# A transformer block on one core: the bias table built earlier, and the last five blocks accumulated onto terms that ScalarE writes into PSUM

## The chip, the core and the metric

The kernel runs on one core of a Trainium2 chip. The core has TensorE (matrix multiply, called PE in the profile, its weight loads PEld), VectorE (DVE), ScalarE (ACT), GpSimd (POOL) and SyncE (SP), which work side by side and wait for each other by semaphores. Data lies in SBUF, in PSUM (eight banks of 512 float32 values in each of 128 partitions, into which TensorE writes) and in device memory, reached by DMA. DMAs are issued by SyncE, ScalarE and GpSimd, each in the order of its queue. The metric is the device time of one execution in microseconds.

## The reference

One block of width 2048 on a sequence of 512 positions, all in float32. With the sizes given, only the first of four mixers is used, attention with a sliding window:

```python
hn = rmsnorm(x, norm_g[0])
q, k, v, gate = split(hn @ swa_w_in)              # 32 query heads, 4 key heads, head size 64
bias = rel_bias[bucket]                           # by distance, 32 buckets, window of 128
scores = q @ k.T * 64 ** -0.5 + bias              # masked to the window
m = maximum(scores.max(-1), sink)
probs = exp(scores - m) / (exp(scores - m).sum(-1) + exp(sink - m))
x = x + ((probs @ v) * silu(gate)) @ swa_w_out
emb = p[0] @ ple_proj
g = sigmoid(rmsnorm(x, ple_norm[0]) @ ple_gate)
x = x + emb * g
return rmsnorm(x, final_g)
```

`rel_bias` holds 32 values for each head; `bucket` maps a distance to one of 32 buckets. The products with `swa_w_out` and `ple_gate` are 512x2048 by 2048x2048.

## The kernel before

**Products.** Each float32 operand is split into a high part of fewer mantissa bits (type float32r) and the rest, and a product is made of three matmuls, high by high, high by low and low by high (`mm3`, lines L121 to L126). ScalarE makes the high part by a copy, VectorE the low part by a subtraction (L107 and L113 for the projections' weights, L709 and L710 later).

**First stage (L186 to L246).** Sixteen steps of k load a slice of x (transposed) and of the first weight columns, split both and accumulate keys, values and two chunks of queries in eight PSUM banks. Between steps 3 and 6 four row tiles of x are read into the four buffers of the pool `whole` (`quarter`), and ScalarE sums their squares (L237). At step 9 the row statistics `rstd1` go through device memory (`rdram`, L241) to a copy `rb` in all partitions (L242); both transfers are on GpSimd's queue. `rb` scales the queries and keys when they leave PSUM (L257, L280).

**The bias table (L318 to L331).** Behind the first stage's last steps GpSimd reads `rel_bias` into a quarter buffer (`misc`), fills a row of 384 values per head by a memset and 17 copies, and writes it to device memory (`tdram`). `load_bias` (L378), on SyncE's queue, reads from there the shifted rows of a group of heads into the tile `bias`. That tile belongs to a pool which takes over the room of the first stage's weights.

**Attention (the loop at L995, 16 steps for each of four key heads).** The order of all engines is written out by hand. In each step TensorE's remaining projection matmuls (`ksteps`) fill the gaps between scores, transposes and weighted sums. SyncE loads the next weights (`W.load`, L101), three buffers ahead, and between them copies weight blocks in device memory (`sum_weights`, L672), onto which GpSimd's queue adds others (L674). Their sums serve the next stage.

**The two large products.** They are computed by a scheme with seven instead of eight block products, on two levels. Of the second (`ple_gate`) the rows of the two lower row tiles (t = 2 and 3) and the columns 0 to 1023 (two chunks jj) come last: product number 4. What has been summed up for them stands, with the wrong sign, in the SBUF tile `s2`, so that their value is product minus `s2`.

**The last five blocks (L1461 to L1553).** Order by hand on all engines. A block (jj, tb) is 24 matmuls into one bank (three for each of 8 slices), and six more that make the embedding `e` in another bank. `block` then has VectorE subtract: `s2 = bank - s2` (L1479); `gated` has ScalarE take the sigmoid (L1302), VectorE multiply by `e` (L1304), add to x (L1308), and an engine sum the squares. The fourth block is cut into two halves of 256 columns. For the last half the subtraction is made on TensorE: two matmuls with a negated identity (`minus`, L1490) bring in the two parts of `-s2` (`less`, L1491 and L1492) ahead of the others (L1468). Banks come from the tags "s" and "p", two each, which the products before have left. Between the blocks stand the final norm of rows already complete and their stores; behind the last one its sum of squares, an inverse root, the scaling of the last row tile and its stores (L1555 to L1585).

Of the kernel before, what the change touches and what calls it, by code (L numbers as in the profile page):

```python
# [11 lines left out]
F32 = mybir.dt.float32  # L12
F32R = mybir.dt.float32r
# [7 lines left out]
P = 128  # L21
KC = D // P
NB = S // P
HEADS = 32
# [9 lines left out]
BUCKETS = 32  # L34
MAX_DIST = 128
WINDOW = 128
PLE = 256
EPS = 1e-6
MASKED = -3.0e38
TOEP = 384  # L40
# [15 lines left out]
def trunk_kernel(ctx: ExitStack, tc: tile.TileContext, a: dict):  # L56
    nc = tc.nc
# [63 lines left out]
    def mm3(ps, sh, sl, mh, ml, first, last, more=False):  # L121


        nc.tensor.matmul(ps, sh, mh, start=first, stop=False, skip_group_check=more)  # L124
        nc.tensor.matmul(ps, sh, ml, start=False, stop=False, skip_group_check=more)  # L125
        nc.tensor.matmul(ps, sl, mh, start=False, stop=last, skip_group_check=more)  # L126
# [3 lines left out]
    ident = const.tile([P, P], F32, name="ident")  # L130
# [24 lines left out]
    def run(gen):  # L155
        for _ in gen:
            pass
# [16 lines left out]

    kinds, upto = [], {"q": 2, "g": 0}
    for kind in "qq" + "qqqqggg" * (KVH - 1) + "ggggggg":
        kinds.append((kind, upto[kind]))
# [6 lines left out]
    for k in range(KC):  # L186
        both = start_pool.tile([P, 2, 768], F32R, tag="w0s", name=f"w0s{k}")
        wh, wl = both[:, 0], both[:, 1]
        xg = start_pool.tile([P, S + 1], F32, tag="xr", name=f"xr{k}")
        nc.sync.dma_start(xg, a["xT"][k * P : (k + 1) * P, :])  # L190
        xr, g1 = xg[:, :S], xg[:, S:]
        w0 = w0s[0] if k == 0 else start_pool.tile([P, 768], F32, tag="w0", name=f"w0_{k}")
        cuts = [slice(512, 768), slice(0, 512)] if k == 0 else [slice(0, 768)]
        for c in cuts[-1:]:
            nc.sync.dma_start(w0[:, c], a["w_first"][k][:, c])
        room = acts if k < KC // 2 else more
        h = room.tile([P, S], F32R, tag="ah", name=f"xh{k}")
        l = room.tile([P, S], F32R, tag="al", name=f"xl{k}")
        nc.scalar.mul(h, xr, g1)
# [12 lines left out]
        qc = [slice(512 + t * P, 512 + (t + 1) * P) for t in range(2)]  # L212
        if f:
            for n, (sw, mx) in enumerate(((wh, h), (wl, h), (wh, l))):
                for t in range(2):
                    nc.tensor.matmul(q_ps[t], sw[:, qc[t]], mx, start=n == 0, stop=False)
        else:
            for t in range(2):
                mm3(q_ps[t], wh[:, qc[t]], wl[:, qc[t]], h, l, f, e)
        for t in range(2):  # L220
            c = slice(t * P, (t + 1) * P)
            mm3(kt_ps[t], wh[:, c], wl[:, c], h, l, f, e)
        for t in range(NB):
            c = slice(t * P, (t + 1) * P)

            for part in "hl" if f else "lh":
                if part == "h":
                    nc.tensor.matmul(v_ps[t], h[:, c], both[:, :, 256:512], start=f, stop=e, skip_group_check=True)  # L228
                else:
                    nc.tensor.matmul(  # L230
                        v_ps[t][:, :256], l[:, c], wh[:, 256:512], start=False, stop=False, skip_group_check=True
                    )
        if 3 <= k < 3 + NB:
            t = k - 3
            xn = quarter(f"xn{t}").rearrange("p k t -> p (k t)")
            nc.sync.dma_start(xn, a["x"][t * P : (t + 1) * P, :])
            nc.scalar.activation(xn, xn, AF.Square, accum_out=ssq1[:, t : t + 1])  # L237
        if k == 9:
            run(rsqrt_mean(rstd1, ssq1, D, "r1"))
            rdram = tc.dram_tile([NB, P], F32, name="rdram")  # L240
            nc.gpsimd.dma_start(rdram.rearrange("t p -> p t"), rstd1)  # L241
# [72 lines left out]
        )  # L314
    split(V[0], values[0])


    misc = quarter("misc")  # L318
    relb, tvec = misc[:HEADS, 1, :BUCKETS], misc[:HEADS, 2, :TOEP]
    nc.gpsimd.dma_start(relb, a["rel"])  # L320
    nc.gpsimd.memset(tvec, MASKED)
    exact = BUCKETS // 2
    bk = bucket_of(np.arange(WINDOW))
    nc.gpsimd.tensor_copy(tvec[:, P - 1 : P - 1 + exact], relb[:, :exact])
    for b in range(exact, BUCKETS):
        d = np.nonzero(bk == b)[0]
        if len(d):
            lo, n = P - 1 + int(d.min()), len(d)
            nc.gpsimd.tensor_copy(tvec[:, lo : lo + n], relb[:, b : b + 1].to_broadcast([HEADS, n]))
    tdram = tc.dram_tile([HEADS, TOEP], F32, name="tdram")  # L330
    nc.gpsimd.dma_start(tdram, tvec)  # L331

    pre.close()
    banks_s.close()
# [247 lines left out]
    def blk(t):  # L582
        return slice(t * P, (t + 1) * P)
# [9 lines left out]
    def block(nm, r, c, jj, m):  # L593
        return a[nm][2 * (c - 1) + jj, 4 * (r - 1) + m]
# [462 lines left out]
    late = pool("late", reuse_waits="tile")  # L1057
# [189 lines left out]
    for at, step in enumerate(OUT):  # L1247
        if at == 20:
            order.close()
        if step == "n":  # L1250
            next(inner)
            step, p = seen, None
            seen += 1
        elif step == "m":
            next(inner2)
            step, p = ("m", seen2), None
# [3 lines left out]
        else:  # L1260
            p, jj, m = step
# [76 lines left out]
    s2, s7 = partial("s2"), partial("s7")  # L1338
# [68 lines left out]
    for at, step in enumerate(PLE, len(OUT)):  # L1407
# [7 lines left out]
        elif step[0] == "e":  # L1415
            while later:
                later.pop(0)()
            p, jj = step[1:]
# [4 lines left out]
        else:  # L1423
            p, jj, m = step
# [32 lines left out]
    ps = psums[3, 1]  # L1457
# [3 lines left out]
    w = [B.get(at_ple["e", 4, jj]) for jj in range(2)]  # L1461
    f = ple_forms.made[4]

    def block(jj, tb, tag, e_tag, c=slice(0, 512), less=None):

        ps = bank(f"last{jj}_{tb}_{c.start}", tag)
        for n, v in enumerate(less or ()):
            nc.tensor.matmul(ps[:, c], minus, v, start=n == 0, stop=False)  # L1468
        for k in range(8):
            fh, fl = f[k // 2]  # L1470
            bh, bl = B.made[at_ple[4, jj] + k // 2]
            mm3(ps[:, c], fh[:, k % 2, blk(tb)], fl[:, k % 2, blk(tb)], bh[k % 2][:, c], bl[k % 2][:, c], k == 0 and not less, k == 7)
        e_ps = embed(2 + tb, w[jj], e_tag, c)
        z = s2[:, jj, tb, c]

        def opened():
            if less:
                return gated(2 + tb, jj, ps[:, c], z, e_ps, c)
            nc.vector.tensor_sub(z, ps[:, c], z)  # L1479
            return gated(2 + tb, jj, z, z, e_ps, c)  # L1480

        return opened


    two = gate(3, 1, ps, e)
    for g in two:
        next(g)
    minus = late.tile([P, P], F32R, name="minus")
    less = [late.tile([P, 256], F32R, name=f"less{n}") for n in range(2)]
    nc.scalar.mul(minus, ident, -1.0)  # L1490
    nc.scalar.copy(less[0], s2[:, 1, 1, 256:])  # L1491
    nc.vector.tensor_sub(less[1], s2[:, 1, 1, 256:], less[0].bitcast(F32))  # L1492
    for g in two:
        next(g)
    split_last(7)
# [44 lines left out]
    g = block(1, 1, "p", "t", slice(0, 256))()  # L1540
    next(g)
    by_gain(3, 0)
    next(g)
# [5 lines left out]
    last = block(1, 1, "s", "o", slice(256, 512), less)()  # L1549
    n += 1  # L1550
    next(last)
    next(last)
# [80 lines left out]
```

## Time and profile before

| | us |
|---|---|
| median of 3 runs | 792.78 |
| lowest and highest | 791.22, 794.69 |
| the profiled execution | 791.03 |
| its span, first to last instruction | 789.3 |

In a list of instructions a row gives the start and the duration in us, the engine, the line of the kernel, the operation, what it writes and reads, shapes, how many were merged (x), and in brackets how long the engine had been idle before and what ended that. In a list of waits a row gives who waited for whom, the total in us, how often, and the longest. In a table by stretches of time the columns are the stretch, the busy time of PE, PEld, DVE, ACT and POOL with their number of instructions, the granted TensorE clock as a share of full speed, the DMA engines' share and GB/s. A trailing q (SPq) marks an engine's issuing part. A matmul's end is modelled, and matmuls overlap, so the distance of two starts tells its cost, not its duration.

### The profile page before, as it was taken

How to read it: one execution, taken by the hardware profiler on the slowest of the kernel's cores; microseconds unless marked ns; L12 is line 12 of the kernel's file. 1: busy time of each engine (PE TensorE's matmuls, PEld its weight loads, DVE VectorE, ACT ScalarE, POOL GpSimd, SP SyncE). 2: the span in 40 equal slices, each digit the busy share in tenths (PEclk: the TensorE clock that was granted, in tenths of full speed). 3: DMA queues.
4: the chain of work that ended last, by engine and by line, in shares of the span. 5: the costliest groups of instructions: out<-in, count | busy, mean ns of one | idle time of the engine just before them, and what ended most of it. 6: DMA issues, size and time to landing. Idle time of an engine off the chain costs nothing.

```text
span 789.3 us, 11284 instructions
## 1 busy us (share of the span) xinstructions
PE 778.5 (99%) x3726; PEld 650.0 (82%) x3726; DVE 623.7 (79%) x1056; ACT 506.5 (64%) x1024; POOL 180.4 (23%) x394
## 2 busy tenths in 40 slices
PE   9999999999999999999999999999999999999995
PEld 8888788888888888888888888888888888888885
DVE  4446468887977788787886798999798988999686
ACT  5632366667666666565665655767788857967465
POOL 0002423544344414444143300200000021101000
PEclk9999999999999999999999999999999999999998
DMA  8797799999999999989997497998778999967833
GB/s 332 282 251 189 259 280 331 297 290 300 305 312 245 309 268 275 278 212 246 294 245 208 136 352 288 245 367 281 249 272 248 365 238 251 255 227 215 256 117 118
DMA packets 50634, 206.99 MB, mean 262 GB/s; under 512 B 7264, under 2 KB 8416, under 8 KB 44208
## 3 DMA queue, kind: packets, MB, share of 16 engines
q1 hardware_dynamic: 40240, 156.15, 54.7%
q0 software_dynamic: 9904, 49.61, 32.8%
q8 instruction: 29, 0.48, 0.2%
q10 hardware_dynamic: 432, 0.52, 0.2%
q14 instruction: 29, 0.24, 0.1%
HBM read 199.38 MB, written 78.69 MB: 352 GB/s over the span
## 4 chain that ended last, share of the span: by engine, by line
PE 92%; DMA 3%; DVE 2%; ACT 1%; issue 1%; SPq 0%; POOL 0%; ACTq 0%; DVEq 0%; POOLq 0%
PE gps L124 7%; PE gps L125 7%; PE gps L126 7%; PE qps L124 6%; PE qps L125 5%; PE qps L126 5%; PE g L125 5%; PE o L124 5%; PE g L124 5%; PE g L126 5%; PE o L125 5%; PE o L126 5%; DMA wraw<-in_w_q 2%; PE vps L228 2%; PE s L400 2%; PE o L522 2%
## 5 line engine op out<-in xcount | busy, mean ns | idle before, releaser
L124 PE MATMUL gps<-xh,whi 128*128 128x512 f32 x256 | 100.5, 393 | 0.0
L125 PE MATMUL gps<-xl,whi 128*128 128x512 f32 x256 | 100.1, 391 | 0.0
L126 PE MATMUL gps<-xh,wlo 128*128 128x512 f32 x256 | 99.9, 390 | 0.0
L113 DVE TENSOR_TENSOR wlo<-wraw,whi 128x1024 fp32r<-128x1024 f32 x60 | 74.6, 1246 | 30.5 <-ACT whi L107 17.2
L502 POOL TENSOR_SCALAR_AFFINE_SELECT own<-r 64x256 fp32r<-64x256 f32 x96 | 60.1, 626 | 162.2 <-DVE r L491 82.7
L126 PE MATMUL qps<-xh,wlo 128*128 128x512 f32 x224 | 87.5, 391 | 0.5 <-DVE wlo L113 0.5
L124 PE MATMUL qps<-xh,whi 128*128 128x512 f32 x224 | 87.7, 391 | 0.0
L125 PE MATMUL qps<-xl,whi 128*128 128x512 f32 x224 | 87.5, 391 | 0.0
L460 ACT ACTIVATE t<-t,sm 128x129 f32<-128x129 f32 x128 | 50.7, 397 | 51.7 <-DVE sm L451 48.8
L107 ACT CAST whi<-wraw 128x1024 fp32r<-128x1024 f32 x60 | 62.2, 1038 | 20.9 <-DMA wraw<-in_w_q 20.9
L710 DVE TENSOR_TENSOR blo<-braw,bhi 128x1024 fp32r<-128x1024 f32 x43 | 52.7, 1229 | 14.9 <-ACT bhi L709 14.9
L709 ACT CAST bhi<-braw 128x1024 fp32r<-128x1024 f32 x43 | 45.0, 1050 | 28.9 <-DMA braw<-in_ple_gate 9.5
L710 DVE TENSOR_TENSOR blo<-ring,bhi 128x1024 fp32r<-128x1024 f32 x48 | 58.3, 1223 | 4.7 <-ACT bhi L709 4.3
L709 ACT CAST bhi<-ring 128x1024 fp32r<-128x1024 f32 x48 | 50.2, 1049 | 17.9 <-PE o L126 14.1
L124 PE MATMUL g<-bhi,fhg 128*128 128x512 f32 x148 | 58.0, 392 | 0.0
L125 PE MATMUL g<-blo,fhg 128*128 128x512 f32 x148 | 57.8, 391 | 0.0
L126 PE MATMUL g<-bhi,flg 128*128 128x512 f32 x148 | 57.7, 390 | 0.0
L126 PEld LDWEIGHTS gps<-xh,wlo 128*128 128x128 f32 x256 | 48.1, 188 | 10.5
L124 PEld LDWEIGHTS gps<-xh,whi 128*128 128x128 f32 x256 | 48.1, 188 | 9.1
L483 ACT CAST r<-pt 128x256 fp32r<-128x256 f32 x64 | 23.8, 371 | 49.5 <-PE pt L478 49.3
L125 PEld LDWEIGHTS gps<-xl,whi 128*128 128x128 f32 x256 | 48.1, 188 | 8.6
L126 PEld LDWEIGHTS qps<-xh,wlo 128*128 128x128 f32 x224 | 42.1, 188 | 10.0 <-DVE wlo L113 1.0
(303 smaller groups left out, 2034.4 us busy)
## 6 DMA issues: line engine op xcount, KB each, us to landing
w_out<-in_w_out POOLq DMA_DIRECT2D x32, 512.0 KB, 9.2
wraw<-in_w_gate_in SPq DMA_DIRECT2D x32, 512.0 KB, 7.7
ring<-w_out SPq DMA_DIRECT2D x32, 512.0 KB, 4.7
wraw<-in_w_q SPq DMA_DIRECT2D x28, 512.0 KB, 9.3
braw<-in_ple_gate SPq DMA_DIRECT2D x22, 512.0 KB, 5.2
ring<-in_w_out SPq DMA_DIRECT2D x18, 512.0 KB, 5.5
ple_gate<-in_ple_gate SPq DMA_DIRECT2D x16, 512.0 KB, 10.0
ple_gate<-in_ple_gate POOLq DMA_DIRECT2D x16, 512.0 KB, 7.9
```

What stands on the lines that cost most here:

```text
L107: nc.scalar.copy(hi, self.raw[i])
L113: nc.vector.tensor_sub(lo, raw, hi.bitcast(F32))
L124: nc.tensor.matmul(ps, sh, mh, start=first, stop=False, skip_group_check=more)
L125: nc.tensor.matmul(ps, sh, ml, start=False, stop=False, skip_group_check=more)
L126: nc.tensor.matmul(ps, sl, mh, start=False, stop=last, skip_group_check=more)
L228: nc.tensor.matmul(v_ps[t], h[:, c], both[:, :, 256:512], start=f, stop=e, skip_group_check=True)
L400: nc.tensor.matmul(s_ps[:, u, : 2 * n], st, key[:, :, first : first + n], start=True, stop=True)
L460: nc.scalar.activation(su, su, AF.Exp, bias=sm[:, u : u + 1], accum_out=sm[:, 2 + u : 3 + u])
L483: nc.scalar.copy(r[:, 0], PT[i])
L502: nc.gpsimd.affine_select(out=cols(own[places[g % 2 ^ low]]), in_=cols(r[here, low].bitcast(F32)), pattern=[[sign * QB, 2], [0, GROUP], [s ...
L709: nc.scalar.copy(hi, raw)
L710: nc.vector.tensor_sub(lo, raw, hi.bitcast(F32))
```

## The change

The bias table becomes a function, `bias_table`, called at step 8 of the first stage; its instructions are the same. In the last five blocks, `seed` has ScalarE write `-s2` into the block's bank ahead of its matmuls, all of which accumulate (no matmul of the block starts the bank anew). The subtraction on VectorE, the negated identity, the two `less` tiles and their two matmuls are gone, and every sigmoid reads PSUM. A seed is issued a block ahead, the two half blocks' seeds together.

```diff
+    def bias_table():
+        misc = quarter("misc")
+        relb, tvec = misc[:HEADS, 1, :BUCKETS], misc[:HEADS, 2, :TOEP]
+        nc.gpsimd.dma_start(relb, a["rel"])
+        nc.gpsimd.memset(tvec, MASKED)
...
+        nc.gpsimd.dma_start(tdram, tvec)
+        return tdram
...
+        if k == 8:
+            tdram = bias_table()
         if k == 9:
             run(rsqrt_mean(rstd1, ssq1, D, "r1"))
...
-    def block(jj, tb, tag, e_tag, c=slice(0, 512), less=None):
-
-        ps = bank(f"last{jj}_{tb}_{c.start}", tag)
-        for n, v in enumerate(less or ()):
-            nc.tensor.matmul(ps[:, c], minus, v, start=n == 0, stop=False)
+    seeded = {}
+
+    def seed(jj, tb, tag, c=slice(0, 512)):
+
+        ps = seeded[jj, tb, c.start] = bank(f"last{jj}_{tb}_{c.start}", tag)
+        nc.scalar.mul(ps[:, c], s2[:, jj, tb, c], -1.0)
+
+    def block(jj, tb, e_tag, c=slice(0, 512)):
+
+        ps = seeded[jj, tb, c.start]
         for k in range(8):
...
-            mm3(ps[:, c], fh[:, k % 2, blk(tb)], fl[:, k % 2, blk(tb)], bh[k % 2][:, c], bl[k % 2][:, c], k == 0 and not less, k == 7)
+            mm3(ps[:, c], fh[:, k % 2, blk(tb)], fl[:, k % 2, blk(tb)], bh[k % 2][:, c], bl[k % 2][:, c], False, k == 7, True)
         e_ps = embed(2 + tb, w[jj], e_tag, c)
         z = s2[:, jj, tb, c]
-            nc.vector.tensor_sub(z, ps[:, c], z)
-            return gated(2 + tb, jj, z, z, e_ps, c)
+        return gated(2 + tb, jj, ps[:, c], z, e_ps, c)
...
-    minus = late.tile([P, P], F32R, name="minus")
-    less = [late.tile([P, 256], F32R, name=f"less{n}") for n in range(2)]
-    nc.scalar.mul(minus, ident, -1.0)
-    nc.scalar.copy(less[0], s2[:, 1, 1, 256:])
-    nc.vector.tensor_sub(less[1], s2[:, 1, 1, 256:], less[0].bitcast(F32))
+    seed(0, 0, "s")
...
     next(root)
-    g = block(0, 0, "s", "o")()
+    seed(1, 0, "s")
+    g = block(0, 0, "o")
...
-    g = block(1, 0, "s", "t")()
+    seed(0, 1, "p")
+    g = block(1, 0, "t")
...
     next(root)
-    g = block(0, 1, "p", "o")()
+    seed(1, 1, "p", slice(0, 256))
+    seed(1, 1, "s", slice(256, 512))
+    g = block(0, 1, "o")
```

What moves, engine by engine; names are the program's tiles, with a number that tells buffers apart. GpSimd's queue from the first stage's end, before:

```order
L241 DMA rdram_481<-rstd1_143 128x4x1
L242 DMA rb_91<-rdram_481 128x512
L674 DMA ple_gate_5_0_0_746<-in_ple_gate 64x2048
L674 DMA ple_gate_5_0_1_747<-in_ple_gate 64x2048
L674 DMA ple_gate_5_0_2_748<-in_ple_gate 64x2048
L674 DMA ple_gate_5_0_3_749<-in_ple_gate 64x2048
L320 DMA misc_715<-in_rel 32x32
L321 MEMSET misc_715 32x384
L324 COPY misc_715<-misc_715 32x16
```

The same queue after the change, from the table's last copies on:

```order
L190 COPY misc_437<-misc_437 32x12
L190 COPY misc_437<-misc_437 32x14
L190 COPY misc_437<-misc_437 32x15
L192 DMA tdram_459<-misc_437 32x384
L261 DMA rdram_503<-rstd1_143 128x4x1
L262 DMA rb_91<-rdram_503 128x512
L679 DMA ple_gate_5_0_0_746<-in_ple_gate 64x2048
```

The table now stands ahead of the statistics' two transfers and of the four accumulating transfers, behind which it stood.

ScalarE ahead of the first of the last blocks, before (`bhi129` is a projection weight's high part, `z1_0` a sigmoid's output, `last7` the high part of a weight of the last product):

```order
L709 CAST bhi128_7605<-braw128_7560 128x1024
L1302 ACTIVATE z1_0_7643<-g1_1_0_6515,rstd2_6389 128x512
L709 CAST bhi129_7623<-braw129_7582 128x1024
L1302 ACTIVATE z1_1_7644<-g1_1_1_6516,rstd2_6389 128x512
L1490 ACTIVATE minus_7647<-ident_83 128x128
L1491 CAST less0_7648<-s2_6395 128x256
L717 CAST last7_7657<-grown86_6702 128x1024
L1311 ACTIVATE z1_0_7643,ssq3_5026<-x1_3_5021 128x512
L1311 ACTIVATE z1_1_7644,ssq3_5026<-x1_3_5021 128x512
L167 ACT_TABLE_LOAD
L167 ACTIVATE rt_r3_7667<-ms_r3_7666 128x2
L1302 ACT_TABLE_LOAD
```

ScalarE at the same place after (`last0_0_0` and `last1_0_0` are PSUM banks):

```order
L714 CAST bhi128_7605<-braw128_7560 128x1024
L1307 ACTIVATE z1_0_7643<-g1_1_0_6515,rstd2_6389 128x512
L714 CAST bhi129_7623<-braw129_7582 128x1024
L1307 ACTIVATE z1_1_7644<-g1_1_1_6516,rstd2_6389 128x512
L1474 ACTIVATE last0_0_0_7647<-s2_6395 128x512
L722 CAST last7_7653<-grown86_6702 128x1024
L1316 ACTIVATE z1_0_7643,ssq3_5026<-x1_3_5021 128x512
L1316 ACTIVATE z1_1_7644,ssq3_5026<-x1_3_5021 128x512
L167 ACT_TABLE_LOAD
L167 ACTIVATE rt_r3_7663<-ms_r3_7662 128x2
L1474 ACTIVATE last1_0_0_7668<-s2_6395 128x512
L1307 ACT_TABLE_LOAD
```

The first seed stands where the negated identity stood, behind two casts and two sigmoids; the second stands behind the square root.

TensorE where the first of the last blocks begins, before, with what an instruction waits for:

```order
L124 MATMUL e_127_0_7634<-bhi_7584,pTh 128x512
L125 MATMUL e_127_0_7634<-blo_7585,pTh 128x512
L126 MATMUL e_127_0_7634<-bhi_7584,pTl 128x512
L124 MATMUL last_0_0_7672<-spare,fhg_00_7425 128x512
L125 MATMUL last_0_0_7672<-spare,fhg_00_7425 128x512
```

and after:

```order
L124 MATMUL e_127_0_7634<-bhi_7584,pTh 128x512
L125 MATMUL e_127_0_7634<-blo_7585,pTh 128x512
L126 MATMUL e_127_0_7634<-bhi_7584,pTl 128x512
L124 MATMUL last_0_0_7647<-spare,fhg_00_7425 128x512 [waits Activation_49]
L125 MATMUL last_0_0_7647<-spare,fhg_00_7425 128x512
```

The order is the same; the block's first matmul now waits for ScalarE. The same wait stands at the first matmul of each of the other four blocks.

More of the change, by code (lines that the diff above doesn't have):

```diff
@@ L173, in rsqrt_mean @@
         nc.vector.tensor_mul(out, y, t)
+    def bias_table():
[3 more added lines that the diff above has]
+        nc.gpsimd.memset(tvec, MASKED)
+        exact = BUCKETS // 2
+        bk = bucket_of(np.arange(WINDOW))
+        nc.gpsimd.tensor_copy(tvec[:, P - 1 : P - 1 + exact], relb[:, :exact])
+        for b in range(exact, BUCKETS):
+            d = np.nonzero(bk == b)[0]
+            if len(d):
+                lo, n = P - 1 + int(d.min()), len(d)
+                nc.gpsimd.tensor_copy(tvec[:, lo : lo + n], relb[:, b : b + 1].to_broadcast([HEADS, n]))
+        tdram = tc.dram_tile([HEADS, TOEP], F32, name="tdram")
+        nc.gpsimd.dma_start(tdram, tvec)
+        return tdram
     kinds, upto = [], {"q": 2, "g": 0}
@@ L315, in trunk_kernel @@
     split(V[0], values[0])
[L318 to L331, printed above, removed]
     pre.close()
@@ L1471, in block @@
             bh, bl = B.made[at_ple[4, jj] + k // 2]
-            mm3(ps[:, c], fh[:, k % 2, blk(tb)], fl[:, k % 2, blk(tb)], bh[k % 2][:, c], bl[k % 2][:, c], k == 0 and not less, k == 7)
+            mm3(ps[:, c], fh[:, k % 2, blk(tb)], fl[:, k % 2, blk(tb)], bh[k % 2][:, c], bl[k % 2][:, c], False, k == 7, True)
         e_ps = embed(2 + tb, w[jj], e_tag, c)
         z = s2[:, jj, tb, c]
-        def opened():
-            if less:
-                return gated(2 + tb, jj, ps[:, c], z, e_ps, c)
-            nc.vector.tensor_sub(z, ps[:, c], z)
-            return gated(2 + tb, jj, z, z, e_ps, c)
-        return opened
+        return gated(2 + tb, jj, ps[:, c], z, e_ps, c)
     two = gate(3, 1, ps, e)
@@ L1539, in trunk_kernel @@
     base, ms, ys, nw, yn = (const.tile([P, 1], F32, name=f"{v}_3") for v in ("base", "ms", "ys", "nw", "yn"))
-    g = block(1, 1, "p", "t", slice(0, 256))()
+    g = block(1, 1, "t", slice(0, 256))
     next(g)
@@ L1548, in trunk_kernel @@
     nc.vector.tensor_mul(x1[1][:, 3, :256], x1[1][:, 3, :256], gain(1)[:, :256])
-    last = block(1, 1, "s", "o", slice(256, 512), less)()
+    last = block(1, 1, "o", slice(256, 512))
     n += 1
```

## The prediction

> **What bounds the kernel now.** I read the page's busy times first, then its chain of waits, then what TensorE itself waited for. These are the three:
>
> ```profile
> PE 778.5 (99%) x3726; PEld 650.0 (82%) x3726; DVE 623.7 (79%) x1056; ACT 506.5 (64%) x1024; POOL 180.4 (23%) x394
> ```
>
> ```profile
> PE 92%; DMA 3%; DVE 2%; ACT 1%; issue 1%; SPq 0%; POOL 0%; ACTq 0%; DVEq 0%; POOLq 0%
> ```
>
> ```profile
> PE warm_ps L145 <- PEq L1623: 0.8, 1, 0.8
> PE qps L126 <- DVE wlo L113: 0.5, 1, 0.5
> PE o L524 <- POOL own L502: 0.3, 1, 0.3
> PE qps L216 <- ACT xh L199: 0.2, 1, 0.2
> ```
>
> TensorE is busy for 99% of the span and its waits add up to 1.8 us. Of these only two (0.5 and 0.3) lie where the change works. So the span is the sum of the matmuls, plus what stands behind the last one:
>
> ```profile
> 780.05 0.28 PE L126 MATMUL e<-bhi,pTl 128*128 128x256 f32 x1
> ```
>
> ```profile
> 780.44 0.42 DVE L1304 TENSOR_TENSOR s<-e,s 128x256 f32<-128x256 f32 x1 [0.37 <-PE e L126]
> ```
>
> The last matmul ends at 780.33. VectorE had idled 0.37 us for it, so the end of about 9 us up to 789.3 hangs on TensorE's last matmul and on nothing earlier. Whatever delays or shortens TensorE's stream before it moves the end one for one; work on VectorE or ScalarE counts only where TensorE waits for it.
>
> **First part, the table.** Rows of GpSimd, of ScalarE's first row sum, of VectorE's first use of the row statistics rb, of SyncE, SyncE's total wait, and TensorE's last matmul of the first stage:
>
> ```profile
> 37.68 0.95 POOL L241 DMA_DIRECT2D rdram<-rstd  x1 [36.30 <-DVE rstd L173]
> ...
> 65.78 0.80 POOL L320 DMA_DIRECT2D misc<-in_rel  x1
> ...
> 78.02 2.08 POOL L329 COPY misc<-misc 32x3 f32<-32x3 f32 x16
> ```
>
> ```profile
> 13.71 1.92 ACT L237 ACTIVATE xn<-xn 128x2048 f32<-128x2048 f32 x1 [1.69 <-DMA xn<-in_x]
> ```
>
> ```profile
> 68.56 1.44 DVE L257 TENSOR_TENSOR rawq<-qps,rb 128x256 f32<-128x256 f32 x4 [4.91 <-PE qps L126]
> ```
>
> ```profile
> 51.55 3.46 SPq L672 DMA_DIRECT2D ple_gate<-in_ple_gate  x4
> 82.36 0.72 SPq L378 DMA_DIRECT2D bias<-tdram  x1
> 83.15 0.87 SPq L101 DMA_DIRECT2D wraw<-in_w_q  x2
> ```
>
> ```profile
> SPq L378 <- DMA tdram<-misc: 27.2, 1, 27.2
> ```
>
> ```profile
> 71.58 0.40 PE L228 MATMUL vps<-w0s,xh 128*128 128x512 f32 x1
> ```
>
> The table takes one small read, a memset, 17 copies and one write, all on GpSimd's queue. It now takes over the quarter buffer of the first row tile, which the square frees at about 15.7. With the 12.2 us from its read to the copies (65.78 to 78.02) and 2.1 us of copies it is complete at about 30, over 7 us ahead of the queue's next item, the statistics' transfer at 37.68. Were the read twice as slow, that transfer would start some 5 us late; its result, rb, is first read at 68.56, and there VectorE had waited 4.91 us for TensorE, not for rb. Price: nothing, covered by GpSimd's 36.3 us of idle time, and if that cover were short, by those 4.9. The accumulating ple_gate transfers behind it on that queue wait for their own copies, past 61. The copies' 2 us beside VectorE's first-stage work fall where that engine is under half busy.
>
> What it frees is SyncE. It stood from 55.0 (51.55 plus 3.46) to 82.36 at the bias load, 27.2 us, with the weight loads queued behind it. The load keeps one other condition, the room of the first stage's weights, which TensorE reads last at 71.58 plus 0.40. So SyncE moves on at about 72, some 10 us sooner. What the late loads cost TensorE:
>
> ```profile
> 87.01 1.05 ACT L107 CAST whi<-wraw 128x1024 fp32r<-128x1024 f32 x1 [13.07 <-DMA wraw<-in_w_q]
> ```
>
> ```profile
> 88.09 1.23 DVE L113 TENSOR_TENSOR wlo<-wraw,whi 128x1024 fp32r<-128x1024 f32 x1 [11.91 <-PE qps L125]
> ```
>
> ```profile
> 88.45 0.40 PE L125 MATMUL qps<-xl,whi 128*128 128x512 f32 x1
> 89.37 0.51 PE L126 MATMUL qps<-xh,wlo 128*128 128x512 f32 x1 [0.53 <-DVE wlo L113]
> ```
>
> Matmuls of 512 columns start 0.23 us apart in this trace (752.34 and 752.57 below). Here the step is 0.92, so 0.69, about 0.7 us, are lost, and ten microseconds more of lead remove all of it. The 0.3 us at own (L502) come from crowded engines some 40 us later; whether earlier loads thin them out the trace doesn't tell, so I count half. Gain: 0.7 plus 0.15 is 0.85, between 0 (another wait takes the place) and 1.0.
>
> **Second part, the seeds.** Five ScalarE writes into PSUM replace four subtractions on VectorE (L1479), one negated identity, one cast and one subtraction for the last half block, and two matmuls (L1468). The two matmuls stand in the chain itself:
>
> ```profile
> 776.50 0.24 PE last L1468 x2
> ```
>
> Gain: 0.24. VectorE's four subtractions (three of 512 columns, one of 256) gain nothing by themselves: the tail above shows it waiting for TensorE. But the seeds bring five waits to TensorE, each at a block's first matmul, with the rest of the stream queued behind it. Before, that matmul needed only a free bank. The first one meets these rows:
>
> ```profile
> 750.63 1.05 ACT L709 CAST bhi<-braw 128x1024 fp32r<-128x1024 f32 x1 [3.69 <-DMA braw<-in_ple_proj]
> 751.58 0.68 ACT L1302 ACTIVATE z<-g,rstd 128x512 f32<-128x512 f32 x1
> 752.16 1.04 ACT L709 CAST bhi<-braw 128x1024 fp32r<-128x1024 f32 x1
> 753.10 0.69 ACT L1302 ACTIVATE z<-g,rstd 128x512 f32<-128x512 f32 x1
> 753.68 0.30 ACT L1490 ACTIVATE minus<-ident 128x128 fp32r<-128x128 f32 x1
> ```
>
> ```profile
> 752.34 0.39 PE L124 MATMUL last<-spare,fhg 128*128 128x512 f32 x1
> 752.57 0.39 PE L125 MATMUL last<-spare,fhg 128*128 128x512 f32 x1
> ```
>
> ```profile
> L570 ACT ACTIVATE gps<-gate x16: 593/602/604, 162.4 to 454.2; 128x512 f32<-128x512 f32 x16
> ```
>
> The seed takes the place of L1490 in ScalarE's queue, behind two casts and two sigmoids that began only when a projection weight landed. So it starts at 753.68. Its price is that of the nearest form in the trace, a 128x512 write from SBUF to PSUM with a constant scale: 0.60 (L570). It is done at 754.28, and TensorE was ready at 752.34. Loss: 1.94 us.
>
> The second seed follows the square root:
>
> ```profile
> 759.52 0.20 ACT L167 ACTIVATE rt_r<-ms_r 128x2 f32<-128x2 f32 x1
> ```
>
> ```profile
> 759.14 0.39 PE L124 MATMUL last<-last,fhg 128*128 128x512 f32 x1
> ```
>
> It ends near 760.2. Alone that would hold TensorE back by 1.1 us, but the first wait has already moved the need from 759.14 to 761.08: covered, and if that cover went, 1.1 us would appear instead. For the third I followed both queues on: it is ready near 766, needed at about 768. The two half seeds are ready near 773.4, needed at about 774.7 and 778.3. So the waits don't add up; the bounds of this term are 1.1 (only the second bites) and 2.6 (the third a little late as well). ScalarE's other work moves back by about 0.6 at the block of 774 and still ends before TensorE does.
>
> **The sum.** 1.94 lost, less 0.24, less 0.85, is +0.85 us. Against the profiled execution: 791.03 (span 789.3, 1.73 around it) becomes 791.9. That execution lies 1.75 below the median of the runs, 792.78; on the median the forecast is 793.6.
>
> **Rivals.** *The lead is lost on the way.* The loads must follow TensorE for 660 us, and at one place they already arrive without slack:
>
> ```profile
> 737.55 1.23 DVE L710 TENSOR_TENSOR blo<-braw,bhi 128x1024 fp32r<-128x1024 f32 x1 [2.50 <-ACT bhi L709]
> ```
>
> ```profile
> 738.83 0.50 PE L125 MATMUL g<-blo,fhg 128*128 128x512 f32 x1
> ```
>
> The split ends at 738.78, TensorE takes it at 738.83. If the loader there runs at its own pace, TensorE cannot arrive a microsecond sooner. Against it: the loads' issues wait for buffers that TensorE's progress frees, so they should move along. Then 1.94 less 0.24, +1.7: 794.5. The same number comes out if the table's move does not free SyncE.
>
> *The first seed is hidden.* ScalarE idled 3.69 us for the projection weight. If that lands two microseconds sooner relative to TensorE, the seed is ready in time, and only the second seed may bite. Then 0 to 1.1 lost, less 1.09: 791.7 to 792.8, taken as 792.0. Against it: nothing in the change touches that load.
>
> *Slower: the clock falls while TensorE waits for the first seed.* The clock by microseconds behind the last matmul, and the warm-up at the start:
>
> ```profile
> 783.00:784.00 1.00, 0.00 (x0) 0.00 (x0) 1.00 (x5) 0.57 (x2) 0.00 (x0) 1.00 0.10 35
> 784.00:785.00 1.00, 0.00 (x0) 0.00 (x0) 0.37 (x1) 0.64 (x1) 0.00 (x0) 0.59 0.94 308
> ```
>
> ```profile
> 0.85 3.79 PE L145 MATMUL warm_ps<-const-bfloat16-1.0 128*128 128x128 bf16 x34 [0.85 <-PEq L1623]
> ```
>
> The granted clock (the column after the engines) fell from 1.00 to half at about 784.2, which is 3.85 us after the matmul that ended at 780.33. In the warm-up 34 matmuls of 128 columns took 0.111 us each against a quarter of 0.23, half speed for 3.8 us, which costs 1.9. It decides from a seed that is 3.85 us late, that is one done at 756.2, which needs the projection weight 1.9 us later than traced. Then 3.85 plus 1.9, less 0.24 and 0.85: +4.7, 797.4. For it: the load's landing isn't steady by construction. Against it: a wait of 1.94 is half of what the row shows. The Trainium skill, in "TensorE: Matmul & The Clock Gate", section "What's actually happening", has the clock fall to half after one idle window of about 3.4 us that runs freely. By that rule a wait of 2 us keeps the full clock, and the trace's 3.85 us agree with it.
>
> **The numbers.** The main case has 0.50 and, with half a microsecond for the seed's landing either way and about 1 for the runs' own scatter, its own range is 792 to 795. The lost lead has 0.22, the hidden seed 0.18, the fallen clock 0.04; 0.03 remain for something slower and 0.03 for something faster that I don't see. About 0.5%, 4 us, is what a measurement of this kernel can tell from no change. The first three cases lie inside it: same 0.90. Slower 0.07, faster 0.03. The range, from the hidden seed less the runs' scatter (they spread 3.5 us) to the lost lead plus it, is 790.5 to 796.2.
>
> **What the profile after would show.** Right: SyncE's bias load near 72 with no 27 us wait, no idle time of TensorE at 89, the table's copies on GpSimd before 37, a wait of TensorE of about 2 us at the first matmul of the last blocks put down to ScalarE's seed, no matmuls of the negated identity, the same 9 us behind the last matmul. Wrong: no such wait, or waits at the other four seeds as well; a clock row below 1.00 near 755; TensorE idle near 739 or in the attention blocks.

## The result, and the profile after

| | median of the runs | lowest to highest | runs |
|---|---|---|---|
| before | 793.62 us | 790.96 to 797.79 | 17 |
| after | 790.84 us | 789.53 to 793.00 | 17 |

The ratio of after to before is 0.9963, 95% interval [0.9951, 0.9976]: the change makes the kernel faster by 0.37%, where I had forecast +0.85 us. That is less than the 0.5% which I had called the least that can be told apart, but the interval lies clear of 1. The second comparison, among the experiments below, gives 0.998 [0.9962, 0.9998]. The spread is smaller too. The execution of before that I had to go by, 791.03, is among the fastest of its kernel; the profiled execution of after, 793.00, is the slowest of its 17.

What TensorE waits for in after (in total, times, longest):

```profile
PE last L124 <- ACT last L1474: 1.9, 1, 1.9
PE warm_ps L145 <- PEq L1627: 0.8, 1, 0.8
PE qps L234 <- ACT xh L217: 0.2, 1, 0.2
```

The waits at 89 and 132 us are gone and the first seed has brought one of 1.9. SyncE's bias load with what follows it, SyncE's wait for the room, and the table on GpSimd:

```profile
72.26 0.71 SPq L383 DMA_DIRECT2D bias<-tdram  x1
73.04 0.87 SPq L101 DMA_DIRECT2D wraw<-in_w_q  x2
```

```profile
SPq L383 <- DVE w0s L226: 9.2, 1, 9.2
```

```profile
15.86 0.70 POOL L181 DMA_DIRECT2D misc<-in_rel  x1 [14.48 <-ACT xn L255]
...
21.78 3.32 POOL L190 COPY misc<-misc 32x3 f32<-32x3 f32 x16
25.41 0.53 POOL L192 DMA_DIRECT2D tdram<-misc  x1 [0.31 <-POOL misc L190]
```

The table is complete at about 26 us, and the loads go out 10 us earlier than before. ScalarE and TensorE at the first of the last blocks, then the clock in stretches of 2 us (the column after the five engines), then the last matmul and the operation behind it:

```profile
749.13 1.05 ACT L714 CAST bhi<-braw 128x1024 fp32r<-128x1024 f32 x1 [2.75 <-DMA braw<-in_ple_proj]
...
752.18 0.60 ACT L1474 ACTIVATE last<-s 128x512 f32<-128x512 f32 x1
```

```profile
752.84 0.50 PE L124 MATMUL last<-spare,fhg 128*128 128x512 f32 x1 [1.89 <-ACT last L1474]
```

```profile
753.00:755.00 2.00, 2.00 (x8) 1.59 (x9) 1.93 (x4) 1.42 (x3) 0.00 (x0) 0.77 0.00 0
755.00:757.00 2.00, 2.00 (x6) 1.63 (x5) 1.97 (x4) 1.38 (x4) 0.00 (x0) 0.50 0.00 0
757.00:759.00 2.00, 2.00 (x9) 1.59 (x8) 0.93 (x7) 1.37 (x3) 0.00 (x0) 0.88 0.00 0
```

```profile
782.03 0.28 PE L126 MATMUL e<-bhi,pTl 128*128 128x256 f32 x1
```

```profile
782.42 0.42 DVE L1309 TENSOR_TENSOR s<-e,s 128x256 f32<-128x256 f32 x1 [1.53 <-PE e L126]
```

The seed took 0.60 and held TensorE for 1.89 us, both nearly as forecast. Then came what I had ruled out for so short a wait: the clock stood at half for 3.4 us (0.23 of 2 us at half rate is 0.92 us in the first row, 2 in the second, 0.48 in the third). Half speed for 3.4 us costs 1.7 us, and this explains why this execution is the slowest of its kernel. The end behind the last matmul is 9 us as before (782.31 to 791.3). So the events that I had named for the right case are all there, and with them one that I had named for the wrong one, a clock row below 1.00 near 755. What the waits don't show is where a gain of 2.8 us comes from.

### The profile page after: what moved, and what is told of

It is laid out like the page before. It is cut to its first block, busy times and chain, and to the rows that moved or that the text cites. A ratio compares the mean times of both kernels' runs of the same rounds, so it can differ in the third digit from the quotient of the medians.

```text
span 791.3 us, 11283 instructions
## 1 busy us (share of the span) xinstructions
PE 779.4 (98%) x3724; PEld 650.8 (82%) x3724; DVE 620.8 (78%) x1051; ACT 508.0 (64%) x1027; POOL 181.7 (23%) x394
## 4 chain that ended last, share of the span: by engine, by line
PE 88%; DVE 4%; DMA 3%; issue 2%; ACT 2%; ACTq 0%; DVEq 0%
PE gps L124 7%; PE gps L125 7%; PE gps L126 7%; PE qps L124 7%; PE qps L125 7%; PE qps L126 7%; PE o L126 5%; PE o L124 5%; PE o L125 5%; PE g L125 2%; PE g L124 2%; PE g L126 2%; PE s L405 2%; PE o L527 2%; PE vps L246 2%
## 5 line engine op out<-in xcount | busy, mean ns | idle before, releaser
L507 POOL TENSOR_SCALAR_AFFINE_SELECT own<-r 64x256 fp32r<-64x256 f32 x96 | 61.9, 645 | 164.8 <-ACT r L488 83.1
```

Of the source, the lines that this page charges most:

```text
L507: nc.gpsimd.affine_select(out=cols(own[places[g % 2 ^ low]]), in_=cols(r[here, low].bitcast(F32)), pattern=[[sign * QB, 2], [0, GROUP], [s ...
```

## The experiments

My theory after the result: the gain of the table's move was sized from one execution of before, which lies below the median, and others lose more to the late weights. The rival: the move brings what I had counted, and the seeds themselves gain.

**Each half alone.** The first kernel has the table early and the last blocks as before, the second the seeds and the table in its old place. The first edit is against before, the second against after; what lies between the lines shown is the table's code, which moves unchanged:

```diff
+    def bias_table():
...
+        if k == 8:
+            tdram = bias_table()
...
-    misc = quarter("misc")
...
-    nc.gpsimd.dma_start(tdram, tvec)
```

> The kernel before with the bias table alone moved into the first stage; the last blocks stay as they were. Theory A (the move's gain was mis-sized): the profiled execution of before, at 791.03 against a median of 793.62, lost little to the late weight loads, and the usual execution loses more. The seeds' two prices then stand (1.9 to 2.05 lost, 0.24 won), and the table alone must bring the measured 2.8 plus 1.7: about 4.5 us, 789.1. Theory B (the seeds gain): the move brings what the two profiles show of it, 0.85 to 1.6, and the time is 792.0 to 792.8. Both expect SyncE's bias load near 72 us, no idle time of TensorE at 89 us and the two matmuls of the negated identity as before.

```diff
-        if k == 8:
-            tdram = bias_table()
...
+    misc = quarter("misc")
...
+    nc.gpsimd.dma_start(tdram, tvec)
```

> The kernel after with the bias table put back where it was; only the seeds are left of the change. Theory A: TensorE waits about 2 us for the first seed and saves 0.24, so the time is 1.7 us above before, 795.3, and if the clock falls behind that wait, about 1.6 more, 796.9. Theory B: the seeds themselves bring 1.2 to 1.9, so 791.7 to 792.4.

On one chip, with a median of 792.39 for before: the table alone 789.88 (0.9965 [0.9952, 0.9977]), the seeds alone 794.41 (1.0023 [1.0009, 1.0038]). The rival falls: the seeds cost 2.0 us, and the table's move wins 2.5. My 4.5 for the table was too much as well; it had been worked out from a single comparison. What TensorE waits for in the profiled execution of the seeds alone, 795.55:

```profile
PE last L124 <- ACT last L1468: 1.5, 1, 1.5
PE o L521 <- DVE r L490: 1.0, 1, 1.0
PE qps L124 <- ACT whi L107: 0.9, 1, 0.9
...
PE qps L126 <- DVE wlo L113: 0.5, 1, 0.5
PE o L523 <- POOL own L501: 0.3, 1, 0.3
```

Beside the seed's 1.5 these are waits between 88 and 135 us, two of them (0.9 and 1.0) at places where the execution that I predicted from had none. There a late table costs something else in each execution.

**After and the table alone, on one chip.** Both are run again, to price the seeds where the table is early.

> The kernel after itself, beside the table alone on the same chip, to price the seeds where the table is early. The seeds alone cost 2.0 us on the kernel before. Theory A (the prices add up): after lies 1.8 to 2.0 above the table alone. Theory C (the wait for the first seed is often shorter when the weights arrive early, or part of it was given back): less than 1.2 above it. In the trace: the first seed's wait is 2.05 us again if it is set by the order of the queues, and differs if it is set by the projection weight's landing; the clock falls behind it again, or not.

> The table alone, as the first run of it, now beside the kernel after on the same chip. 2.5 us below before if the move's gain holds from chip to chip.

Before 792.46, after 791.42 (0.998 [0.9962, 0.9998]), the table alone 789.89 (0.9959 [0.994, 0.9978]). The move's gain holds, 2.6 us. The seeds cost 1.5 on top of it, between the two theories' bounds; by the means (791.17 and 789.88) it is 1.3.

**The first seed's wait from execution to execution.** After was profiled once more:

> One more look at the kernel after: a wait of 1.3 to 2.1 us at the first seed, none at 85 to 140 us; the clock falls behind the wait where it is near 2 us (theory D), and not where it is 1.5 or less.

The block's first matmul in the two later executions of after:

```profile
752.74 0.50 PE L124 MATMUL last<-spare,fhg 128*128 128x512 f32 x1 [1.16 <-ACT last L1474]
```

```profile
751.42 0.50 PE L124 MATMUL last<-spare,fhg 128*128 128x512 f32 x1 [0.46 <-ACT last L1474]
```

With the first profile's 1.89 the wait is 1.9, 1.2 and 0.5, below the expected 1.3 to 2.1 in two of three. In the second execution TensorE had lost 0.5 us to a late load at 738 us and so came later to a seed that stood at the same time (752.09, in the first profile 752.18). In the third the projection weight landed earlier and the seed began at 750.78. The mean, 1.2, less the two matmuls' 0.24, makes 1.0; the runs say 1.3 to 1.5. The clock did not fall behind 1.2 or 0.5; where it falls, as in the first profile, its 1.7 us come on top.

**The seeds moved to where ScalarE is idle.** In the next two kernels the first seed, or the first two, stand ahead of the casts that wait for the projection weight:

```diff
+            if (p, jj) == (3, 1):
+                seed(0, 0, "s")
+                seed(1, 0, "s")
             w = B.get(at)
...
-    seed(0, 0, "s")
...
-    seed(1, 0, "s")
```

The two lines of `seed(1, 0, "s")` are those of the second kernel alone; the definition of `seed` moves up with the call.

> The kernel after, with the first seed issued on ScalarE ahead of the casts and sigmoids that wait for the projection weight, where ScalarE idles 2.75 us. Theory A: the wait of TensorE at the first matmul of the last blocks (2.05 us) goes, and with it the fall of the clock to half that the profile of after shows behind it (1.6 us, if it is usual). The second seed's cover goes too, and it may cost up to 1.1. So 788.8 to 789.9 without the fall in the usual execution of after, 787.2 to 788.3 with it. Theory B (the wait at the first seed is not on the path that sets the end, or is made up later): 790.8, as after.

> As the run with the first seed early, and the second seed with it, ahead of the projection weight's casts. Theory A: no seed holds TensorE back any more, so the seeds cost nothing and save the two matmuls' 0.24: 0.24 below the table alone, 788.8 if that is 789.1. If the second seed was covered anyway, this run and the one with the first seed early are equal; if it was not, this one is faster by up to 1.1. Theory B: 790.8, as after.

They take 789.56 (0.9963 [0.995, 0.9977]) and 789.98 (0.9963 [0.9948, 0.9979]), beside 789.88 for the table alone on the same chip: no difference between the three. The first lies in theory A's range; the second lies above theory A's 788.8, which took the table alone at 789.1, and below theory B's 790.8. Moving the second seed as well brings nothing that the runs show. With one seed early the second one bites, for half of the 1.1 us that the prediction had as its bound:

```profile
757.77 0.50 PE L124 MATMUL last<-last,fhg 128*128 128x512 f32 x1 [0.48 <-ACT last L1407]
```

With both early TensorE waits for no seed at all. So the seeds' cost is their place in ScalarE's queue, and without it they win no more than their 0.24, which the runs can't tell. These versions and the table alone lie below both kernels.

**Where the late table costs.** Before was profiled twice more, and a kernel run in which SyncE's bias load stands behind the first weight loads, while the table's code stays where it was:

```diff
     for n in range(SUM_FIRST):
         sum_weights(n)
-    load_bias(0)
     blocks = KVH * STEPS
...
         for v in range((SUM_START - SUM_FIRST) // 4):
             sum_weights(SUM_FIRST + n * ((SUM_START - SUM_FIRST) // 4) + v)
+    load_bias(0)
     for e in range(2):
```

> The kernel before, looked at again, to see where an execution nearer its median loses time against the one profiled at 791.03. Theory A: between 85 and 140 us, at matmuls that wait for the split of a late weight, as in the run with the seeds alone, where 1.1 and 0.7 were lost at 88 to 90 and 2.0 at 122 to 135. Rival: elsewhere, at the start (the clock's rise), in the loads of 690 to 750 us, or in the tail.

> One more look at the kernel before. Theory P: what lies between its executions is the time lost at 88 to 90 and at 121 to 138; ScalarE's weight cast near 117 waits 1.5 us or more for its load each time, and TensorE loses the more, the longer it waits. Rival: the executions differ elsewhere.

> The kernel before with its table made where it was, but the load of the bias moved on SyncE's queue behind the first weight loads. Theory A1 (what the table's move brings comes from SyncE's queue, which no longer stands for 27 us ahead of the weight loads): this edit brings it too, 2 to 2.8 us below before, with no idle time of TensorE at 88 to 90 and at 122 to 134. Theory A2 (it comes from GpSimd, which no longer makes the table at 65 to 82 us while the first block's other transfers wait behind it): GpSimd still makes it here, and the time is that of before, or above it if the later bias is waited for.

To compare executions I take three matmuls, the same in every kernel (the 414th, 564th and 670th of TensorE's stream, ahead of which no edit changes a matmul), and the time between their starts. In before and in the table alone they are:

```profile
85.21 0.39 PE L126 MATMUL qps<-xh,wlo 128*128 128x512 f32 x1
...
118.01 0.39 PE L124 MATMUL qps<-xh,whi 128*128 128x512 f32 x1
...
140.21 0.39 PE L126 MATMUL qps<-xh,wlo 128*128 128x512 f32 x1
```

```profile
85.60 0.39 PE L126 MATMUL qps<-xh,wlo 128*128 128x512 f32 x1
...
117.50 0.39 PE L124 MATMUL qps<-xh,whi 128*128 128x512 f32 x1
...
138.88 0.39 PE L126 MATMUL qps<-xh,wlo 128*128 128x512 f32 x1
```

| execution | its time | 85 to 118 | 118 to 140 | lost in both, against the last row |
|---|---|---|---|---|
| before, as predicted from | 791.03 | 32.81 | 22.20 | 1.74 |
| before, profiled again | 791.33 | 32.49 | 22.98 | 2.20 |
| before, a third time | 792.55 | 32.95 | 23.24 | 2.92 |
| seeds alone (table late) | 795.55 | 33.96 | 24.08 | 4.77 |
| bias load later | 791.08 | 31.90 | 23.01 | 1.64 |
| GpSimd held (below) | 792.60 | 31.90 | 24.02 | 2.65 |
| all eight with the table early and nothing held | 789.6 to 796.5 | 31.90 | 21.37 | 0 |

The eight executions with an early table agree here to 0.01 us: TensorE loses nothing. Of the five with a late table each loses something else, 1.64 to 4.77. The mean of the three of before is 2.3, and 2.5 to 2.6 is what the runs show. The one I predicted from has the smallest loss of these three, and even it lost 1.74, twice what I had counted as gain. So the losses lie where theory A of the second profile and theory P of the third have them; the third execution loses another 0.8 us at 702 to 705, as their rivals have it in part.

The kernel with the later bias load splits the two stretches: with SyncE no longer blocked the first is 31.90, but the second stays at 23.01. It took 790.80 (0.9984 [0.9961, 1.0007], twelve runs between 789.33 and 795.69), so its times show no gain. It tells less about GpSimd than was meant: on that engine's queue the table came out behind one more transfer and was made at 78.9 to 93.2 us in place of 65.8 to 80.9. So neither of its two theories holds alone. ScalarE's weight cast near 117 us tells what is late in the second stretch; in before, in its third profile, and in the table alone:

```profile
117.07 1.05 ACT L107 CAST whi<-wraw 128x1024 fp32r<-128x1024 f32 x1 [1.59 <-DMA wraw<-in_w_q]
```

```profile
118.04 1.05 ACT L107 CAST whi<-wraw 128x1024 fp32r<-128x1024 f32 x1 [2.35 <-DMA wraw<-in_w_q]
```

```profile
114.82 1.04 ACT L107 CAST whi<-wraw 128x1024 fp32r<-128x1024 f32 x1
```

ScalarE stands for the load; VectorE stands for ScalarE's cast, with the softmax and the weighted sum's operand `r` behind it in its queue; and TensorE waits for `r` at 121 to 124 us in every late execution but one, and for `own`, which GpSimd makes from `r`, at 132 to 135 in all of them. The exception is the execution that I predicted from: its 0.83 us lie behind `own` alone, at 132 and 137. The cast's wait and the loss in the second stretch are 1.59 and 0.83 there, 2.70 and 1.61, 2.35 and 1.87 in the other two of before, 3.54 and 2.71 in the seeds alone, so the loss grows with the wait, though not strictly; in the eight with an early table both are nothing. The first of these rows was in the profile that I had.

**GpSimd held.** Why is that load late, 35 us after SyncE moved on? It is not issued late: it goes out at 104.87 us in before and at 104.58 in the table alone, behind the first copies of `DV`. It takes longer. In the chain of waits of before it is this row, and in the table alone it has landed when ScalarE comes to it at 114.82, after 10.2 us at most:

```profile
104.87 12.18 DMA wraw<-in_w_q
```

In before, GpSimd's queue reaches its accumulating transfers of 512 KB (L674, L678 with the table early) at 98 to 102 us, in the table alone at 89 to 95:

```profile
98.42 0.79 POOL L674 DMA_DIRECT2D small<-in_w_out  x1
...
101.45 0.77 POOL L674 DMA_DIRECT2D small<-in_w_out  x1 [0.80 <-DMA small<-in_w_out]
```

```profile
89.32 0.77 POOL L678 DMA_DIRECT2D small<-in_w_out  x1
...
95.08 0.78 POOL L678 DMA_DIRECT2D small<-in_w_out  x1 [3.11 <-DMA small<-in_w_out]
```

There are three of them in each. They stand behind a first one that waits for SyncE's copy of the same block; that copy stands in SyncE's queue behind the bias load and goes out at 84.06 us in before and at 74.09 in the table alone. This is how SyncE's wait makes GpSimd late. At 98 to 102 the three meet SyncE's copies of the half differences of the values (`DV`) and the next weight loads. To test this the table stays early, SyncE stays free, and GpSimd alone is held back ahead of these transfers by a difference that it makes eleven times:

```diff
-        nc.gpsimd.tensor_sub(v[lower], values[n][lower], values[n - 1][lower])
+        for _ in range(11 if n == 1 else 1):
+            nc.gpsimd.tensor_sub(v[lower], values[n][lower], values[n - 1][lower])
```

> The table alone in the first stage, but GpSimd makes its first half difference of the values eleven times instead of once, so that it reaches the accumulating transfers behind the differences some 8 to 10 us later, near 98 us as in the kernel before; SyncE is free at 72 us as in the table alone. Theory P (two effects: SyncE's block costs 0.9 to 1.7 at 88 to 90 us; the transfers that GpSimd issues late then crowd the copies of DV and the weight loads at 100 to 118 us, and cost 0.7 to 2 at 121 to 138): no wait of TensorE at 88 to 90, ScalarE's weight cast near 117 waits for its load again, TensorE waits at 121 or 132, and the time is 790.5 to 791.9. Theory S (SyncE's block alone counts): 789.9 and no wait at 121 to 138.

The whole gain is gone: 792.13, beside 792.37 for before on the same chip (0.9999 [0.9985, 1.0013]); the table alone had run on another, 2.5 and 2.6 below before. The profile shows it where theory P has it: 31.90 in the first stretch, 24.02 in the second, and these waits of TensorE:

```profile
PE o L527 <- DVE r L496: 1.0, 1, 1.0
...
PE o L529 <- POOL own L507: 0.3, 1, 0.3
```

The price is more than my bound of 2 (24.02 less 21.37 is 2.65); GpSimd came to these transfers at 102.2, some 4 us later still than in before. So the run shows the mechanism, and not its size in before, where the second stretch lost 0.83 to 1.87. The edit has a rival of its own: the copies of `DV` read the differences that it holds back. But the first two groups of these copies went out at 101.66 and 105.47 us, in the table alone at 101.35 and 105.83, and the weight load between them at 104.13. It was again the flight that was longer:

```profile
104.13 13.99 DMA wraw<-in_w_q
```

From 104 to 118 us, while this load is under way, GpSimd's own queue (`q0`) took this share of the DMA engines' time, in before, in the table alone and with GpSimd held:

```profile
q0 software_dynamic: 275, 1.73, 61.8%
...
q0 software_dynamic: 82, 0.54, 21.6%
...
q0 software_dynamic: 309, 2.01, 73.3%
```

The transfers issued between 98 and 112 us, with KB of each and median us from issue to landing, in the same order:

```profile
DV<-diffs SPq DMA_DIRECT2D x7, 128.0 KB, 11.7
```

```profile
DV<-diffs SPq DMA_DIRECT2D x9, 128.0 KB, 3.4
wraw<-in_w_q SPq DMA_DIRECT2D x2, 512.0 KB, 7.4
```

```profile
DV<-diffs SPq DMA_DIRECT2D x8, 128.0 KB, 10.3
wraw<-in_w_q SPq DMA_DIRECT2D x2, 512.0 KB, 11.8
```

Where the accumulating transfers go out at that time, a copy of `DV` lands after 10 to 12 us in place of 3.4, and the second weight load of these rows, behind the copies in SyncE's queue, after 11.8 in place of 7.4. (The landing of the first, the load of the rows above, is not in this list.)

**The clock behind a longer wait.**

```diff
-        nc.scalar.mul(ps[:, c], s2[:, jj, tb, c], -1.0)
+        for _ in range(3 if (jj, tb) == (0, 0) else 1):
+            nc.scalar.mul(ps[:, c], s2[:, jj, tb, c], -1.0)
```

> The kernel after with the first seed written three times instead of once, so that TensorE waits 1.2 us longer for it, 2.6 to 3.3 us. Theory D (the clock falls where about 2 us of waiting lie within one span of 3.4 us, as in the profiled execution of after): it falls to half for 3.4 us in most executions, and the time is 1.2 plus about 1.6 above after, 793.5 to 794.2. Rival (the price of a wait is the wait, the fall was one execution's): 792.6, with the clock at 1.00 around 755.

It takes 793.58 (1.0012 [0.9995, 1.0028], ten runs from 791.29 to 796.48), the figure of theory D, though the interval holds the rival's 792.6 as well. Seven of the ten show a mean clock of 0.992 to 0.995, three 0.996 or 0.997; after shows 0.996 to 0.998 in all runs but its first profiled one (0.994). The mean clock alone is a rough sign: the kernel with the later bias load, which has no seeds, shows 0.993 and 0.994 in two of its twelve runs, and why is open. But the times of the seven (793.30 to 796.48) lie above those of the three (791.29 to 792.45). In the profiled execution, 796.48, the clock behind a wait of 3.2 us was:

```profile
753.00:755.00 2.00, 0.00 (x0) 0.00 (x0) 1.97 (x3) 1.94 (x5) 0.00 (x0) 0.82 0.00 0
755.00:757.00 2.00, 1.97 (x5) 1.59 (x6) 1.97 (x4) 1.99 (x4) 0.00 (x0) 0.50 0.00 0
...
761.00:763.00 2.00, 2.00 (x10) 1.61 (x10) 1.58 (x3) 0.00 (x0) 0.00 (x0) 0.98 0.78 278
```

Half speed from 754.28 (0.82 of 2 us is 0.72 at half) to 761.08, that is 6.8 us, twice 3.4. So the clock's fall behind this wait is shown for one execution, and for seven of ten it is inferred.

## Why the prediction was wrong, and where it was right

- **What failed: the gain of the table's move, put at 0.85 us.** The prediction says of the 0.3 us at `own` that "whether earlier loads thin them out the trace doesn't tell, so I count half", and bounds the gain by 0 and 1.0. In the very execution it was read from, the late table cost 1.74: 0.91 up to 118 us where I had 0.7, and 0.83 behind it where I had 0.15. The second term was mis-sized twice over. First, its 0.3 is the idle time of the list of waits, whereas at 89 us I had gone by the distance of starts. By the starts the step behind `own` is 1.05 us (131.21 to 132.26) in before and 0.44 (130.70 to 131.14) in the table alone, so 0.61 were lost there, and 0.26 in the same way at 137:

```profile
131.21 0.56 PE L522 MATMUL o<-r,V 128*128 128x256 f32 x2
132.03 0.39 PE L524 MATMUL o<-own,DV 128*128 128x256 f32 x1 [0.26 <-POOL own L502]
132.26 0.43 PE L400 MATMUL s<-k,q 128*128 128x288 f32 x2
```

```profile
130.70 0.48 PE L526 MATMUL o<-r,V 128*128 128x256 f32 x2
131.02 0.28 PE L528 MATMUL o<-own,DV 128*128 128x256 f32 x1
131.14 0.43 PE L404 MATMUL s<-k,q 128*128 128x288 f32 x2
```

Second, all of it goes and not half, because I followed the freed queue, SyncE's, only as far as its first loads. GpSimd's accumulating transfers behind the bias load move with it, and I did not ask what they collide with; the cast at 117 us that stood 1.59 for its load was the sign of it.
- **The second failure: one execution taken for the kernel.** I noted that the profiled execution lies 1.75 below the median and added my net to the median unchanged. The term that I was sizing differs between the executions of before: 1.74, 2.20 and 2.92 in three of them, in the order of their times, against 0 with an early table. So the gain that I read from one of the fastest could not be that of the median, where the runs show 2.5 to 2.6. The measured 790.84 lies in the stated range only because the range allows for the runs' scatter; the sign of the change was wrong.
- **Right: the seeds.** 1.94 and -0.24 make 1.7. The runs show 2.0 on the kernel before and 1.3 to 1.5 with the early table. The wait itself was 1.89, 1.16 and 0.46 in three executions; the seed's 0.60 and its place behind two casts and two sigmoids were as read. In the third the weight landed early, which is the rival of the hidden seed in part. The second seed's cover was real: without the first wait it cost 0.48.
- **Right in the main: that the lead is kept.** TensorE's lead of 1.74 stays up to 690 us. On the rest of the way to the last blocks late loads cost between 0 and 1.2 us in the eight executions with an early table, 0.7 in the mean, and between 0 and 0.8, 0.4 in the mean, in the six in which the table or GpSimd is late. At 738, the place that the rival of the lost lead names, four of the eight lose 0.3 to 0.8 and none of the six more than 0.1. So a part of the lead can be lost again there; the means lie too close together to price it.
- **Wrong: the threshold for the clock.** The rival asked for 3.85 us of waiting. The clock fell after 1.89 in one of the three profiled executions of after; the mean clock of its other runs, 0.996 to 0.998, speaks against many more.
- **Right: the table on GpSimd costs TensorE nothing, and the end behind the last matmul is unchanged.**

The parts add to -2.6 and +1.4, -1.2 us; the second comparison has -1.0 by the medians and -1.7 by the means, the first had -2.8. Before's median was 793.62 in the first and 792.4 in the three later ones, which is most of the difference; why before was slower there stays open, and so does why one execution with a late table loses 1.7 us and another 4.8.

## What to carry to other kernels

When a wait on a queue goes, follow everything that was queued behind it, on every queue that depends on it, to the place where it now runs, and ask what it used to collide with there. A term that is itself a race of transfers should be read from several executions, or sized with the spread of the runs: the 0.3 us of one list of waits was 0.83 by the distance of starts, and with the late table that stretch lost 0.8 to 2.7 from execution to execution. Where an operation on an idle engine must be ready for TensorE, its place in that engine's queue decides its cost before its duration does.

## What was not expected of the hardware

The clock falls after less idle time than I thought, and not after every wait of the same length. In after it fell at 754.08 and came back at 757.48, and TensorE had been idle for 1.89 us (750.95 to 752.84) of the 3.4 us ahead of the fall, 55%; a wait of 1.50 in the seeds alone, which may have lain across two windows, and one of 1.16 in after's second profile left it at 1.00. With 3.2 us of waiting it fell, as far as the mean clocks tell, in about seven executions of ten, and in the profiled one for two spans of 3.4 us instead of one. The Trainium skill, in "TensorE: Matmul & The Clock Gate", section "What's actually happening", describes a window of about 3.4 us that runs freely and lets the clock fall after an idle one. The two lengths of 3.4 and 6.8 us agree with that window; read as a window that is idle throughout, the rule does not, since 55% was enough here. What share is enough, above 34% (1.16 of 3.4, if all of that wait lay in one window) and up to 55%, is not settled by these runs.
